# Decode attention of the sample rows: between the blocks of the gating branch instead of behind the heads of the recurrence

## The chip, the cores and the metric

The kernel runs on one core of one Trainium2 chip, in one launch. The metric is the device time of a run in microseconds. Engines are called by the profile's names: PE is TensorE (PEld its weight loads), DVE is VectorE, ACT is ScalarE, POOL is GpSimd, and SP is SyncE, whose queue issues most of the DMAs.

## What is computed

The reference is one step of a decoder layer with three parallel branches over one input projection. A prompt of 1024 tokens and 8 sample rows (one new token for each of 8 sequences) go through the same layer:

```python
h = rms(x, norm_g); proj = h @ w_in
aq, ak, av, az, bu, bv, bz, cq, cf, ci, cz = split(proj)
o_a = dilated attention          # windows (128,1), (512,4), (2048,16), mixed by softmax denominators
o_b = bu * (tril(W_s) @ layernorm(bv) + b)      # gating in chunks of 128
o_c = rms(HGRN2 recurrence of cq, cf, ci)       # 6 heads, state 128 x 128
x + concat(o_a * silu(az), o_b * silu(bz), o_c * silu(cz)) @ w_out
```

For the sample rows, the attention is a decode step: each of the 8 new queries meets up to 129 keys of each of the three patterns, gathered by stride from a cache of 2048 rows, and its own new key:

```python
kg, vg = kk[:, idx], vv[:, idx]                 # idx = W + t - arange(win // dil + 1) * dil
s = einsum('bthe,btnhe->bthn', q, kg); p, lse = softmax_stats(s)
out = combine over the patterns of einsum('bthn,btnhe->bthe', p, vg)
```

It needs the projections of the sample rows and the caches, and nothing of the other two branches. Its result is needed by the output projection of the sample rows alone.

## The kernel before, in words

Everything is unrolled. The order on each engine and each DMA queue is not written by hand: the framework takes the program's order as a priority, runs a simulated timeline, and lets an engine take the first instruction that is ready in it. The result is a fixed order for each engine and each queue; on the chip an engine that waits holds up all that is behind it in that order. Tiles come from pools by tag; each tag has a fixed number of buffers, and a new tile waits until an older one of the tag has been read for the last time.

The stages in the order of the program are: input norm and transposes; `attention()` (three rounds of two head pairs); `hgrn()`, the recurrence; `sgu()`, the gating branch; `out_proj(U)`, four blocks of 256 output columns with eight row tiles of 128 tokens each.

`hgrn()` (from line 780) goes over three pairs of heads. Per pair it projects the values (`c_proj_i`), the queries and forget gates of the first head (`c_proj_qf`, also of the second head further down) and the output gates z (`c_proj_z`). Per head follow `c_head`, which computes the prompt's recurrence (three levels of decay-weighted products by `levels`, tiles T, masked into `cmat` by lines 722 to 729), `c_step` (line 763), which advances the state of the 8 sample rows, and `decode` (line 923). A projection collects 24 matmuls in one of two PSUM banks (tag "proj"); for q and z a bank is emptied by `gate`, whose first instruction is on DVE (line 152). So projections of the next head or pair fill PE while DVE works on the current head, as long as DVE comes to the gates.

`decode(p)` handles one of six pairs of attention heads. Per half of the batch it loads the queries, broadcast to all partitions (`dqb`, line 947), and three tiles of gathered keys (`dk`, line 935; one more small load for the new key, line 937). DVE multiplies (line 949) and reduces (line 950) each tile into the score tile `dsc`. A maximum follows over partitions by way of two small transposes (`pmx`, `pmb`), then exponential, multiplicities, denominator (`pdn`), the weighted sum of six value tiles on PE (`pda`, 48 matmuls), a transposition (`pdt`) and the last multiply into `ysT` (line 978). The tiles dqb, dk, dv and the copy for the transposition have the tag "pq" with five buffers, which `c_step` (vb, ss), `sgu` (two rows of norm weights) and `out_proj` (xr, line 1036) use as well. The score tile has one buffer, tag "dsc", cleared by two memsets on POOL (lines 943, 944). PSUM tiles of decode share the one bank of tag "tr" with c_step and a few transposes of sgu.

`sgu()` (line 811) transposes and masks W_s with `triu`, adds up bias terms `bT`, projects v in two blocks (`bv`, row statistics in `st6`, which has the tag "dsc" too), normalises, and then runs four blocks of projections, bz 0, bu 0, bz 1, bu 1 (lines 885 to 899), with the mixing matmuls (`mx`) after each bu. Each block begins with `load_w` (line 192): four loads of 256 KB on SP's queue, a rounding copy on ACT and a subtraction on POOL (line 206) for the low half.

`out_proj` loads the columns `y` and `yb` from DRAM, `xr` per row tile, and adds the PSUM result to xr on DVE (line 1054). PE's sample rows (`pos`, `pon`) need ysT of all six decodes.

Of the kernel before, what the change touches and what calls it, by code (L numbers as in the profile page):

```python
# [18 lines left out]
P = 128  # L19
# [3 lines left out]
NT = S // P  # L23
# [11 lines left out]
OFF_BU, OFF_BV, OFF_BZ = 3072, 3584, 4096  # L35
# [4 lines left out]
NEG = -3.0e38  # L40
# [51 lines left out]
def hybrid_step(tc, ins, outs, parts=("A", "D", "B", "C", "O"), dbg=None):  # L92
    nc = tc.nc
# [8 lines left out]
    with tc.tile_pool(name="const", bufs=1) as cp, tc.tile_pool(name="sb", bufs=1) as sb, \  # L102
# [14 lines left out]
        def s2b(nm, dt=F32, shape=(P, 512)):  # L117
            return sb.tile(list(shape), dt, tag="s2b", name=nm, bufs=N_S2B)
# [4 lines left out]
        def small(nm, n, p=P, dt=F32, bufs=2, tag=None):  # L123
            return sb.tile([p, n], dt, tag=tag or f"sm{n}", name=nm, bufs=bufs)
# [94 lines left out]
        for t in (0, NT, *range(1, NT)):  # L219
# [15 lines left out]
            for j in range(2):  # L235
                ps = p_st(f"tr0_{t}_{j}").rearrange("p (a b) -> p a b", a=4)
                for i in range(4):
                    k = 4 * j + i
# [541 lines left out]
        def hgrn():  # L780
            cm = sb.tile([P, 1024], F32, tag="mask", name="cmat", bufs=1)
            lmask, dmask = cm[:, 640:856].bitcast(BF16), cm[:, 856:872].bitcast(BF16)
            nc.gpsimd.dma_start(lmask, ins["lmask"])
            nc.gpsimd.dma_start(dmask, ins["dmask"])
            nc.gpsimd.memset(cm[:, 512:640], 0.0)
            At = [(cm[:, 256 * j:256 * j + 256], cm[:, 512 + 64 * j:576 + 64 * j]) for j in range(2)]
            for hp in range(3):
                V = c_proj_i(hp)
                a = c_proj_qf(2 * hp)
                Z = c_proj_z(hp)  # L790
                c_head(2 * hp, *a, V[0], Z[0], At, lmask, dmask)
                c_step(2 * hp, *a)
                decode(2 * hp)
                a = c_proj_qf(2 * hp + 1)
                c_head(2 * hp + 1, *a, V[1], Z[1], At, lmask, dmask)
                c_step(2 * hp + 1, *a)
                decode(2 * hp + 1)

            n = HC * NS
            sq = pq("ssq", (P, n))  # L800
            nc.scalar.activation(sq, osT.rearrange("p h b -> p (h b)"), AF.Square)
            pn = p_tr("pns")
            mm(pn[:, :n], ones, sq, True, True)
            nc.scalar.activation(sq, pn[:, :n], AF.Ln, scale=1.0 / P, bias=eps)
            nc.scalar.activation(sq, sq, AF.Exp, scale=-0.5)
            nc.vector.tensor_tensor(osT, osT, sq.rearrange("p (h b) -> p h b", b=NS), ALU.mult)
            nc.vector.tensor_tensor(osT, osT, gn[:, :, None].to_broadcast([P, HC, NS]), ALU.mult)
            nc.vector.tensor_tensor(ysT[:, 10:16, :], osT, zsT, ALU.mult)


        def sgu():
            triu = small("triu", P, bufs=1, tag="kg")
            nc.scalar.dma_start(triu, ins["triu"])
            wn = wk("wn", (P, 8, P))
            nc.scalar.dma_start(wn, ins["sgu_w"][0].rearrange("g t s -> t g s"))
# [19 lines left out]

            vraw = [inp(f"vraw{g}", (P, 2, CB)) for g in range(4)]
            v_s = s2b("v_s", shape=(NS, CB))
            st6 = small("st6", NT * 12, bufs=1, tag="dsc").rearrange("p (t a b) -> p t a b", t=NT, a=2)
            for j in range(2):
                blk = load_w([(OFF_BV + j * NW, NW)], f"bv{j}")  # L840
                st = proj_nat_s(blk, f"bv{j}")
                nc.scalar.copy(v_s[:, j * NW:(j + 1) * NW], st)
                for g in range(4):
                    ps = p_proj(f"pbv{j}_{g}").rearrange("p (a b) -> p a b", a=2)
                    for i in range(2):
                        proj_nat(blk, 2 * g + i, ps[:, i, :])
                    dst = vraw[g][:, :, j * NW:(j + 1) * NW]
                    nc.scalar.copy(dst, ps)
                    for i in range(2):
                        nc.vector.bn_stats(st6[:, 2 * g + i, j, :], dst[:, i, :])  # L850
# [16 lines left out]
            for nm, op in (("sgu_ln_g", ALU.mult), ("sgu_ln_b", ALU.add)):  # L867
                t = pq(f"s_{nm}", (NS, CB))
# [16 lines left out]
            U = []  # L885
            for j in range(2):
                U += [inp(f"u{j}_{i}") for i in range(2)]
                for nm, off in (("bz", OFF_BZ), ("bu", OFF_BU)):
                    blk = load_w([(off + j * NW, NW)], f"{nm}{j}")
                    for i in range(2):  # L890
                        for c in range(3):
                            ps = p_proj(f"p{nm}{j}_{i}_{c}")
                            proj_T(blk, i * P, c, ps[:, :TC])
                            us = U[2 * j + i][:, c * TC:(c + 1) * TC]
                            if nm == "bz":
                                gate(us, ps[:, :TC], f"bzt{j}_{i}_{c}")
                            else:
                                nc.vector.tensor_tensor(us, ps[:, :TC], us, ALU.mult)
# [21 lines left out]
            cns[nm] = cp.tile(list(ins[nm].shape), F32, name=nm)  # L920
            tc.keep_in_program_order(nc.scalar.dma_start(cns[nm], ins[nm]))

        def decode(p):

            ROWS = ((P, 1920, 1), (96, 1536, 4), (96, 0, 16))
            ch = slice(p * P, (p + 1) * P)
# [11 lines left out]
                        n += 1  # L938
                    yield kind, n, t

            scw = small(f"dsc{p}", 138, bufs=1, tag="dsc").rearrange("p (k a) -> p k a", k=3)
            sc = scw[:, :, 0:16]
            nc.gpsimd.memset(sc, NEG)
            nc.gpsimd.memset(scw[:, :, 16:], 0.0)
            for bb in range(2):
                qb = dk(f"dqb{p}_{bb}")
                nc.sync.dma_start(qb, qkv_d[0, 4 * bb:4 * bb + 4, ch].partition_broadcast(P))
# [118 lines left out]
        if "A" in parts:  # L1066
            attention()
        if "C" in parts:
            hgrn()
        if "B" in parts:  # L1070
            U = sgu()
        if "O" in parts:
            out_proj(U)

# [23 lines left out]
```

## Time and profile before

| | |
|---|---|
| median of 3 runs | 1285.43 us (1284.22 to 1287.84) |
| the profiled execution, its own time | 1283.54 us |
| its span from the first to the last instruction | 1281.8 us |
| mean granted TensorE clock | 0.977 |
| share of the span: PE, DVE, ACT, POOL busy | 94%, 71%, 52%, 23% |
| chain that ended last | PE 72%, DVE 16%, DMA 5% |
| DMA | 114.17 MB, 89 GB/s |

The span is cut into stages by what runs in them: attention until some 560 us, the recurrence's heads until 996 us, the gating branch until 1084 us, then the output projection. Stages overlap at their edges. Busy time of an engine says little by itself; the gaps of PE and what ended them say where time is lost. The granted clock is the share of full speed at which PE was allowed to run in a stretch.

### The profile page before, as it was taken

What the parts mean: (1) busy time and instruction counts of PE and PEld (TensorE: products, weight loads), DVE (VectorE), ACT (ScalarE), POOL (GpSimd) and SP (SyncE); (2) the same over time, 40 slices, a digit from 0 to 9 for tenths busy, and PEclk for the clock granted to TensorE, in tenths of its full rate; (3) what the DMA queues carried; (4) which work ended last, traced back from release to release, by engine and by line L of the source; (5) the groups of instructions that cost most, each with busy time, mean ns of one, the idle gap of its engine ahead of it and who ended that gap; (6) DMA issues with size and microseconds to landing.
All of it is one profiled execution on the core that took longest, in us unless ns stands there. A gap on an engine that the chain in (4) does not pass through costs nothing.

```text
span 1281.8 us, 27727 instructions
## 1 busy us (share of the span) xinstructions
PE 1206.7 (94%) x10610; PEld 1119.9 (87%) x10610; DVE 914.1 (71%) x2425; ACT 669.8 (52%) x1512; POOL 290.1 (23%) x272
## 2 busy tenths in 40 slices
PE   3899999999999998998999889998999999999998
PEld 2899888998899988987988878887989899899998
DVE  4845888668876786789897898989796534654643
ACT  5445554765547565575445554665443252455543
POOL 4431201312203221122012121111011254122221
PEclk9999999999899998999999889999999999999999
DMA  7241222312223141142253514424253224621110
GB/s 224 68 136 34 65 55 79 108 37 66 71 67 100 42 117 52 25 111 84 67 146 92 131 46 139 127 80 112 81 149 97 84 75 137 194 80 47 62 47 29
DMA packets 165044, 114.17 MB, mean 89 GB/s; under 512 B 13944, under 2 KB 158992, under 8 KB 164912
## 3 DMA queue, kind: packets, MB, share of 16 engines
q1 hardware_dynamic: 157520, 110.28, 29.4%
q10 hardware_dynamic: 6816, 1.54, 0.6%
q8 instruction: 83, 1.36, 0.4%
q0 software_dynamic: 576, 0.58, 0.3%
q14 instruction: 49, 0.40, 0.1%
HBM read 84.47 MB, written 22.09 MB: 83 GB/s over the span
## 4 chain that ended last, share of the span: by engine, by line
PE 72%; DVE 16%; DMA 5%; issue 3%; ACT 3%; SPq 0%; POOL 0%; ACTq 0%; POOLq 0%; DVEq 0%
PE po L100 15%; PE pqk L100 10%; PE pv L100 9%; PE paz L100 5%; PE pi L100 4%; PE pbu L100 4%; PE pbz L100 4%; PE pcz L100 4%; PE pc L100 3%; PE pbv L100 3%; PE st L100 3%; DMA dk<-in_cache_k_dram 2%; PE s L100 2%; DVE T L647 1%; DVE T L649 1%
## 5 line engine op out<-in xcount | busy, mean ns | idle before, releaser
L100 PE MATMUL pqk<-wh_qk,h 128*128 128x256 f32 x768 | 156.6, 294 | 9.1 <-DVE h L243 4.4
L100 PE MATMUL pc<-h,wh_cqf 128*128 128x344 f32 x576 | 144.6, 331 | 10.3 <-DVE cz L152 8.8
L100 PE MATMUL po<-woh,yl 128*128 128x256 f32 x512 | 144.5, 283 | 0.0
L100 PE MATMUL po<-woh,yh 128*128 128x256 f32 x512 | 144.1, 282 | 0.3 <-ACT yh L1046 0.3
L100 PE MATMUL po<-wol,yh 128*128 128x256 f32 x512 | 143.9, 281 | 0.0
L100 PEld LDWEIGHTS pqk<-wh_qk,h 128*128 128x128 f32 x768 | 127.9, 198 | 17.0 <-DVE h L243 5.0
L100 PEld LDWEIGHTS pc<-h,wh_cqf 128*128 128x128 f32 x576 | 102.1, 194 | 13.4 <-DVE cz L152 9.7
L100 PE MATMUL pqk<-wl_qk,h 128*128 128x256 f32 x384 | 112.1, 292 | 0.0
L100 PEld LDWEIGHTS po<-woh,yl 128*128 128x128 f32 x512 | 96.6, 189 | 3.0 <-issue 1.7
L100 PEld LDWEIGHTS po<-woh,yh 128*128 128x128 f32 x512 | 96.3, 188 | 2.1 <-ACT yh L1046 2.1
L100 PEld LDWEIGHTS po<-wol,yh 128*128 128x128 f32 x512 | 96.5, 189 | 0.0
L100 PE MATMUL pc<-h,wl_cqf 128*128 128x344 f32 x288 | 95.3, 333 | 0.0
L455 DVE CUSTOM_DVE_ANT_0 s<-s,masks 128x512 f32<-128x512 f32 (+2 forms) x144 | 77.6, 576 | 19.4 <-PE s L100 18.6
L100 PE MATMUL pi<-wh_ci,h 128*128 128x256 f32 x384 | 79.1, 301 | 10.5 <-DVE cmat L722 8.1
L100 PEld LDWEIGHTS pqk<-wl_qk,h 128*128 128x128 f32 x384 | 75.7, 197 | 1.4 <-issue 0.2
L100 PEld LDWEIGHTS pi<-wh_ci,h 128*128 128x128 f32 x384 | 65.1, 204 | 13.6 <-ACT dsc L962 5.4
L100 PE MATMUL pv<-wh_v,h 128*128 128x256 f32 x384 | 75.2, 287 | 1.0 <-ACT den L516 1.0
L100 PE MATMUL pcz<-h,wh_cz 128*128 128x344 f32 x288 | 71.2, 325 | 0.2 <-DVE q L152 0.2
L100 PE MATMUL paz<-h,wh_az 128*128 128x344 f32 x288 | 68.9, 323 | 0.0
L1047 DVE TENSOR_TENSOR yl<-yb,yh 128x512 fp32r<-128x512 f32 x44 | 30.3, 692 | 52.6 <-ACT yh L1046 52.6
L100 PEld LDWEIGHTS pv<-wh_v,h 128*128 128x128 f32 x384 | 61.1, 189 | 3.1 <-ACT st L493 1.1
L1046 ACT CAST yh<-yb 128x512 fp32r<-128x512 f32 x64 | 39.5, 620 | 42.7 <-PE po L100 41.9
(389 smaller groups left out, 3586.5 us busy)
## 6 DMA issues: line engine op xcount, KB each, us to landing
wro<-in_w_out_dram SPq DMA_DIRECT2D x32, 256.0 KB
wr_qk<-in_w_in_dram SPq DMA_DIRECT2D x48, 128.0 KB
wr_cqf<-in_w_in_dram SPq DMA_DIRECT2D x48, 128.0 KB
dk<-in_cache_k_dram SPq DMA_DIRECT2D x24, 192.0 KB
dv<-in_cache_v_dram SPq DMA_DIRECT2D x24, 192.0 KB
xt<-in_x_prompt_dram SPq DMA_DIRECT2D x8, 512.0 KB
xr<-in_x_prompt_dram SPq DMA_DIRECT2D x32, 128.0 KB
out_o_yp_dram<-xr SPq DMA_DIRECT2D x32, 128.0 KB
```

The costliest lines, as they stand in the source:

```text
L100: nc.tensor.matmul(out, lhsT=lhsT, rhs=rhs, start=start, stop=stop)
L455: nc.vector.tensor_tensor_reduce(out=ps[:, :w], in0=ps[:, :w], in1=nmask[:, S - n + c:S - n + c + w], op0=ALU.add, op1=ALU.max, scale=1.0, ...
L647: nc.vector.tensor_tensor(K.rearrange("p (n w) -> p n w", w=w), g3[:, :, w - 1:w].to_broadcast([P, 4 * n, w]), h3, ALU.subtract)
L649: nc.vector.tensor_tensor(Q[:, 0:3], g4[:, 1:4], g4[:, 0:3, :, w - 1:w].to_broadcast([P, 3, n, w]), ALU.subtract)
L1046: nc.scalar.copy(yh[:, sl, :], y)
L1047: (nc.gpsimd if piece == 0 else nc.vector).tensor_tensor(yl[:, sl, :], y, yh[:, sl, :].bitcast(F32), ALU.subtract)
```

## The change

The calls of `decode` leave `hgrn()`. In `sgu()`, decode 0 and 1 are called ahead of the two bv blocks, and decode 2 to 5 ahead of the blocks bz 0, bu 0, bz 1, bu 1. Decodes of odd number take their score tile from 138 unused columns of the tile `cmat`, which `hgrn` now returns, instead of the one buffer of "dsc"; the two memsets of the scores go from POOL to DVE; `triu` moves to a buffer of the tag "s2b" (two buffers, also used for kT, csq, v_s, ms and tb), and `st6` to the buffer of "kg" that triu had.

```diff
--- before.py
+++ after.py
@@ -790,11 +790,9 @@
                 Z = c_proj_z(hp)
                 c_head(2 * hp, *a, V[0], Z[0], At, lmask, dmask)
                 c_step(2 * hp, *a)
-                decode(2 * hp)
                 a = c_proj_qf(2 * hp + 1)
                 c_head(2 * hp + 1, *a, V[1], Z[1], At, lmask, dmask)
                 c_step(2 * hp + 1, *a)
-                decode(2 * hp + 1)
 
             n = HC * NS
             sq = pq("ssq", (P, n))
@@ -806,10 +804,11 @@
             nc.vector.tensor_tensor(osT, osT, sq.rearrange("p (h b) -> p h b", b=NS), ALU.mult)
             nc.vector.tensor_tensor(osT, osT, gn[:, :, None].to_broadcast([P, HC, NS]), ALU.mult)
             nc.vector.tensor_tensor(ysT[:, 10:16, :], osT, zsT, ALU.mult)
-
-
-        def sgu():
-            triu = small("triu", P, bufs=1, tag="kg")
+            return cm[:, 872:1010]
+
+
+        def sgu(wide):
+            triu = s2b("triu", shape=(P, P))
             nc.scalar.dma_start(triu, ins["triu"])
             wn = wk("wn", (P, 8, P))
             nc.scalar.dma_start(wn, ins["sgu_w"][0].rearrange("g t s -> t g s"))
@@ -835,8 +834,9 @@
 
             vraw = [inp(f"vraw{g}", (P, 2, CB)) for g in range(4)]
             v_s = s2b("v_s", shape=(NS, CB))
-            st6 = small("st6", NT * 12, bufs=1, tag="dsc").rearrange("p (t a b) -> p t a b", t=NT, a=2)
+            st6 = small("st6", NT * 12, bufs=1, tag="kg").rearrange("p (t a b) -> p t a b", t=NT, a=2)
             for j in range(2):
+                decode(j, wide)
                 blk = load_w([(OFF_BV + j * NW, NW)], f"bv{j}")
                 st = proj_nat_s(blk, f"bv{j}")
                 nc.scalar.copy(v_s[:, j * NW:(j + 1) * NW], st)
@@ -885,7 +885,8 @@
             U = []
             for j in range(2):
                 U += [inp(f"u{j}_{i}") for i in range(2)]
-                for nm, off in (("bz", OFF_BZ), ("bu", OFF_BU)):
+                for jj, (nm, off) in enumerate((("bz", OFF_BZ), ("bu", OFF_BU))):
+                    decode(2 + 2 * j + jj, wide)
                     blk = load_w([(off + j * NW, NW)], f"{nm}{j}")
                     for i in range(2):
                         for c in range(3):
@@ -920,7 +921,7 @@
             cns[nm] = cp.tile(list(ins[nm].shape), F32, name=nm)
             tc.keep_in_program_order(nc.scalar.dma_start(cns[nm], ins[nm]))
 
-        def decode(p):
+        def decode(p, wide):
 
             ROWS = ((P, 1920, 1), (96, 1536, 4), (96, 0, 16))
             ch = slice(p * P, (p + 1) * P)
@@ -938,10 +939,10 @@
                         n += 1
                     yield kind, n, t
 
-            scw = small(f"dsc{p}", 138, bufs=1, tag="dsc").rearrange("p (k a) -> p k a", k=3)
+            scw = (wide if p % 2 else small(f"dsc{p}", 138, bufs=1, tag="dsc")).rearrange("p (k a) -> p k a", k=3)
             sc = scw[:, :, 0:16]
-            nc.gpsimd.memset(sc, NEG)
-            nc.gpsimd.memset(scw[:, :, 16:], 0.0)
+            nc.vector.memset(sc, NEG)
+            nc.vector.memset(scw[:, :, 16:], 0.0)
             for bb in range(2):
                 qb = dk(f"dqb{p}_{bb}")
                 nc.sync.dma_start(qb, qkv_d[0, 4 * bb:4 * bb + 4, ch].partition_broadcast(P))
@@ -1066,9 +1067,9 @@
         if "A" in parts:
             attention()
         if "C" in parts:
-            hgrn()
+            wide = hgrn()
         if "B" in parts:
-            U = sgu()
+            U = sgu(wide)
         if "O" in parts:
             out_proj(U)
```

## Rows read from the trace of the kernel before

**Rows 1.** The page's first part: busy us, share of the span, instructions.

```profile
PE 1206.7 (94%) x10610; PEld 1119.9 (87%) x10610; DVE 914.1 (71%) x2425; ACT 669.8 (52%) x1512; POOL 290.1 (23%) x272
```

**Rows 2.** Busy time by stage: stretch, length, PE, PEld, DVE, ACT, POOL, PEclk, DMA share, GB/s.

```profile
565.00:645.00 80.00, 71.75 (x780) 65.76 (x778) 72.31 (x206) 45.82 (x114) 18.19 (x16) 0.94 0.34 93
645.00:717.00 72.00, 68.69 (x724) 63.15 (x724) 60.58 (x166) 38.69 (x85) 14.88 (x12) 1.00 0.43 120
...
996.00:1084.00 88.00, 88.00 (x623) 81.48 (x624) 34.54 (x62) 28.02 (x57) 37.82 (x29) 1.00 0.29 88
565.00:996.00 431.00, 399.24 (x4390) 365.66 (x4389) 369.64 (x1100) 224.67 (x542) 73.67 (x62) 0.96 0.38 105
```

**Rows 3.** PE's waits, 480 to 1110 us: who waited for whom, us, times, longest.

```profile
PE pc L100 <- DVE cz L152: 8.8, 3, 3.7
PE pi L100 <- DVE cmat L722: 8.1, 2, 5.0
...
PE pss_bv L100 <- DVE q L152: 3.3, 1, 3.3
...
PE pss_ci L100 <- DVE q L152: 1.4, 2, 0.9
PE pmx L955 <- DVE dmx L953: 1.3, 1, 1.3
...
PE pcz L100 <- POOL wl_cz L206: 0.7, 1, 0.7
```

**Rows 4.** Busy time of three 10 us windows inside heads 0, 2 and 4.

```profile
600.00:610.00 10.00, 6.42 (x45) 5.21 (x44) 9.97 (x28) 8.32 (x18) 7.55 (x4) 0.80 0.32 91
...
750.00:760.00 10.00, 5.54 (x28) 5.57 (x29) 9.88 (x33) 6.08 (x14) 3.81 (x3) 0.66 0.36 106
890.00:900.00 10.00, 6.17 (x38) 4.69 (x39) 9.87 (x29) 6.49 (x15) 3.35 (x3) 0.66 0.32 107
```

**Rows 5.** Decode's DVE instructions, by tile: ns min/median/max, first and last start.

```profile
L949 DVE TENSOR_TENSOR dk<-dk,dqb x36: 670/682/694, 577.4 to 945.5; 128x512 f32<-128x512 f32 x12, 97x512 f32<-97x512 f32 x12, 96x512 f32<-96x512 f32 x12
L950 DVE TENSOR_REDUCE dsc<-dk x36: 664/673/686, 579.6 to 947.3; 128x8 f32<-128x512 f32 x12, 97x8 f32<-97x512 f32 x12, 96x8 f32<-96x512 f32 x12
...
L967 DVE RECIPROCAL dmx<-pdn x6: 239/242/257, 617.2 to 963.3; 128x16 f32<-128x16 f32 x6
L978 DVE TENSOR_TENSOR ysT<-ysT,dmx x6: 157/159/162, 638.3 to 985.0; 128x8 f32<-128x8 f32 x6
```

**Rows 6.** Busy time of the instructions on dv, 560 to 1010 us, their sum.

```profile
sum 450.00, PE 13.55 PEld 8.07; mean PE 0.30 PEld 0.18
```

**Rows 7.** POOL's wait before the memset of the scores: us, times, longest.

```profile
POOL dsc L943 <- PE pda L100: 55.4, 4, 22.4
```

**Rows 8.** The same DVE operation of `levels` at two moments (start, us).

```profile
604.47 1.08 DVE L654 TENSOR_TENSOR T<-T,dec 128x64 f32<-128x64 f32 x1
...
758.77 0.20 DVE L654 TENSOR_TENSOR T<-T,dec 128x64 f32<-128x64 f32 x1
```

**Rows 9.** Two users of the tag "s2", by tile: first and last start.

```profile
L827 ACTq DMA_DIRECT2D bT<-in_sgu_b_dram x8: 472/604/1053, 973.4 to 980.4; - x8
...
L649 DVE TENSOR_TENSOR T<-G x72: 331/352/1460, 565.7 to 955.7; 128x192 f32<-128x192 f32 x72
```

**Rows 10.** SP's queue around decode 5, a landing time in the chain, and xr's addition.

```profile
928.32 1.46 SPq L947 DMA_DIRECT2D dqb<-qkv_scr  x1
...
966.78 0.38 SPq L935 DMA_DIRECT2D dv<-in_cache_v_dram  x1
...
981.03 8.18 SPq L1036 DMA_DIRECT2D xr<-in_x_prompt_dram  x3
...
1079.86 10.75 SPq L1015 DMA_DIRECT2D yb<-y_scr  x7
...
644.36 5.16 DMA dk<-in_cache_k_dram
...
L1054 DVE TENSOR_TENSOR xr<-xr,po x32: 400/421/422, 1091.7 to 1278.5; 128x256 f32<-128x256 f32 x32
```

## The prediction

> **What bounds the kernel now.** The first thing read is the page's busy line: TensorE (PE) works 1206.7 us of a 1281.8 us span [rows 1], so the most that any reordering can win without removing work is the 75 us in which PE idles, plus what it loses at the lower clock. The table by stage comes next, to see where those 75 us lie [rows 2]. From 565 to 996 us, the heads of the recurrence, PE works 399.24 of 431 us and the granted clock is 0.96; from 996 to 1084 us, the gating branch, PE is never idle while VectorE (DVE) works only 34.54 of 88 us. The reader should see two things there: the recurrence holds 31.8 us of PE idleness, with DVE busy 369.64 of 431 us; and the loss is uneven. The stretch of head 0 (565 to 645) loses 8.3 us, that of head 1 (645 to 717) 3.3 us. PE's own list of waits then says what ended the idleness [rows 3]: 8.8 us at the start of a first head of a pair (projection matmuls behind the DVE gate of z), and in the middle of such a head 8.1 + 3.3 + 1.4 = 12.8 us, where a projection's PSUM bank waits for DVE. Three 10 us windows at these middles show DVE at 9.9 of 10 us, PE at 5.5 to 6.4 us, and a granted clock of 0.80, 0.66 and 0.66 [rows 4]. So this stage is bound by DVE in bursts, and PE pays for it twice, by idling and by running at the lower of its two levels, 1.2 instead of 2.4 GHz, afterwards.
>
> **The change part by part.**
> *DVE work leaves the recurrence.* Per decode six multiplies of 0.682 and six reductions of 0.673 us [rows 5], 8.1 us, and ten small operations between 0.16 and 0.24 us like the last column multiply and the reciprocal, about 2 us: 10 us a decode, 60 us in six. Five of six go behind the last head; the sixth ran during the last head and decode 0 will too. In head 0 the decode's multiplies and reductions ran ahead of the middle burst, on a DVE that was saturated from there to the burst. Without them DVE reaches the gate that PE waits for some 8 us earlier, and the 12.8 us fall on three such bursts, 4.3 us each on average, so I take them all as gone, and the 1.3 us that PE waited for a decode's maximum [rows 3]. The bounds are 1.3 us (only the decode's own wait) and 31.8 us (every idle microsecond of the stage).
> *Clock.* At 0.80, 0.66 and 0.66 of 10 us, PE was at the lower level for 4.0 + 6.8 + 6.8 = 17.6 us. If all of it fell on matmuls, half of it, 8.8 us, was lost; where it fell on idle time, nothing. I take 3 us. The sum for the recurrence is -12.8 - 1.3 - 3 = -17 us.
> *The start of each pair stays.* The 8.8 us behind the gate of z come before the decode's first multiply, so they are not in my sum.
> *PE work is moved, not removed.* The 288 matmuls of the weighted sum take 13.55 us of PE [rows 6], the transposes and the denominator some 3 us. They leave a stage and enter another, both limited by PE most of the time: nothing in the sum. In the gating branch PE has no idle time to hide them in; they lengthen it by the 16 us by which they shorten the recurrence.
> *Score clearing goes from POOL to DVE, and a second score tile is used.* POOL stood 55.4 us in four waits for the previous decode's matmuls [rows 7]; behind it in POOL's queue are the low halves of the weights. PE's list names POOL for 0.7 us [rows 3], so what this frees is priced at nothing; it is covered by PE's other work. On DVE twelve clears enter; by the nearest DVE row, the reciprocal of 0.242 us, they are 2.9 us of a DVE that idles 53 of 88 us. If the second tile's predecessor is still being read, a clear on DVE blocks all DVE behind it, the gates of bz above all; with two tiles in turn the reader is two decodes back, so I take nothing.
> *Port sharing.* In the window where POOL ran four subtractions in 7.55 us [rows 4], DVE's 128x64 multiply took 1.08 us, against 0.20 us elsewhere [rows 8]. In the gating branch POOL is busy 37.82 of 88 us against 73.67 of 431 [rows 2], so the moved multiplies, which read two operands, will be stretched more often; at worst 36 x 0.88 = 32 us, still within DVE's idle 53 us, so the sum gets nothing. The Trainium skill (SBUF — State Buffer, section "SBUF: two separate sides") says that a VectorE operation with two SBUF inputs and a GpSimd operation that reads SBUF take a shared port pair in turn, each for its whole length. That rule speaks against this change, since it moves such operations to where GpSimd is busier; the trace agrees with it by the 1.08 us, and by it the sum would still be the same.
> *Other tiles.* triu moves to the tag of kT and csq and so behind the last head's, and the statistics tile st6 leaves the score tile's tag, whose last reader was decode 5. Both are priced at nothing: PE has the bz block to work on meanwhile; if that cover is gone, the cost is the load of triu, some 5 us like a cache load's [rows 10].
> *Loads.* Each decode has two query loads, twelve cache loads and four small ones on SP's queue, and 15 tiles pass through the five "pq" buffers. Buffers of a tag seem to be given out in program order: bT, ready from the start, was loaded at 973.4 us, after the last T tile of the same tag was begun at 955.7 [rows 9]. Then decode 0 starts once the sample step of the last head has its buffers, and the output projection's xr tiles, of the same tag, come behind decode 5. In the old order decode 5 issued its first load at 928.32 and its last at 966.78, 38.5 us apart, finished at 985.0 [rows 5], and xr was loaded from 981, 110 us before its first use [rows 10]. That lead vanishes. Weight loads are issued on the same SP queue; with six raw buffers they run a block and a half ahead, which covers a decode load that waits for its buffer.
> *Is there room for six?* The third tile of the output projection needs xr 0, since its matmuls have two PSUM banks and the first must be emptied. A tile takes (1278.5 - 1091.7) / 31 = 6.0 us [rows 10]; so xr must land 12 us after 1084, and be issued 5 us before, the time that a cache load took to land [rows 10], so at 1091. From 928 that is 163 us, plus the 13 us of PE work of five decodes that no longer lie ahead: 29 us for each of six. If the sample step of the last head, which had waited for decode 4's buffers, runs up to 30 us earlier, it is 34 us. I take 37 us for decode 0 under the last head's DVE load, 33 for decode 1, and 27 for the rest, where DVE is idle more than half the time: 178 us in all against 176 to 206. It just fits, without margin.
> *Price behind the recurrence.* Between nothing and the 50 us that six decodes of 38.5 us would be late (231 - 176 = 55). I take 4 us, nearer to nothing since it fits, for a start of the output projection that is crowded: SP already needs 10.75 us there to issue seven y loads [rows 10].
> *Sum.* -17 + 4 = -13 us. The profiled execution took 1283.54 us, so 1270.5; the median of the runs shown is 1.9 us above it. I say 1271.
>
> **The rivals.**
> 1. *Slower: the decodes don't fit.* The place is the third tile of the output projection, where PE waits for xr behind decode 5 in the "pq" buffers, while SP's queue is full of y loads. It decides if a decode takes more than about 34 us on average. At the 38.5 us seen before it is late by 25 to 55 us; with 30, the time is 1283.5 - 17 + 30 = 1296. For it: the only pitch that the trace shows is 38.5 us, each decode passes one-buffer tiles ("tr", "dmx"), and its start is held by the last sample step. Against: that pitch was measured with DVE busy 9 of 10 us, and behind 996 us DVE is mostly free.
> 2. *No change: the backlog is not the decode's.* The heads' own level and mask operations fill DVE in the bursts, and another of them takes the place of each decode operation; then only 1.3 us and a little clock are won and 2 to 4 are paid behind: 1283 to 1286. For it: at the waits themselves DVE runs level operations, not decode ones, some stretched by POOL. Against: odd heads, with the same operations, lose little.
> 3. *All of the stage's idleness goes.* With POOL free and the sample step early, DVE has 60 us more, and the starts of the pairs relax too: 1283.5 - 31.8 = 1252.
>
> **How the numbers follow.** Forecast 0.5, rival 1 0.23, rival 2 0.15, rival 3 0.12. A measurement of this kernel tells about 0.3% from no change, 3.9 us. Faster: rival 3 and nearly all of the forecast's cases (some end within 3.9 us): 0.61. Same: rival 2 mostly, and the edge of the forecast: 0.16. Slower: 0.23. The range reaches down to rival 3's 1252 and up to 1294, leaving out the upper half of rival 1 and what lies beyond rival 3; the forecast's own range is 1260 to 1280.
>
> **What would show it.** In the changed profile the middles of heads 0, 2 and 4 should show PE busy 9 to 10 of 10 us at a clock near 1.0, the recurrence should be 25 to 35 us shorter (17 from waits, the rest moved PE work) and the gating branch some 14 us longer, with PE still without idle time. POOL's wait for the weighted sum should be gone. Decode 5's last load should be issued before PE begins the output projection's third tile. I am wrong if PE's list of waits has a new entry of over 5 us at the output projection's DVE addition or its xr loads (rival 1), or if the waits behind DVE in the middle of the first heads stand as before (rival 2).

## The result, and the profile after

The changed kernel takes 1344.86 us, median of four runs (1342.36 to 1348.83), against 1284.83 us for the kernel before in the same comparison (1280.58 to 1287.84): a ratio of 1.048, 95% interval 1.0452 to 1.0507. It is 60 us slower. The forecast was 1271, the range ended at 1294, and slower had a chance of 0.23. The profiled execution took 1348.83 us; its span is 1347.0 us and the mean granted clock 0.953 (before: 1281.8 us and 0.977).

First the page's busy line and two lines of its picture in 40 slices, of the kernel after; the first answers to [rows 1].

```profile
PE 1223.3 (91%) x10610; PEld 1131.3 (84%) x10610; DVE 917.8 (68%) x2437; ACT 673.4 (50%) x1512; POOL 292.8 (22%) x260
...
PE   4899999998999989988998799889999953899999
...
PEclk9899999999999989989999999999999875799999
```

The matmuls are the same 10610, but PE is busy 16.6 us longer and its span is 65.2 us longer, so 48.6 us are new idleness. The picture shows where: one hole in slices 33 to 35, where the granted clock falls to 0.5 of full speed.

A table by stage makes that exact. The stages are cut at the first matmul of the recurrence (`pi`), of the gating branch (`pbv`) and of the output projection, and at the last matmul. Columns as in [rows 2]: stretch, length, busy us of PE, PEld, DVE, ACT and POOL, granted clock, DMA share, GB/s. The kernel before, cut in the same way:

```profile
462.80:896.00 433.20, 398.27 (x3904) 365.74 (x3902) 362.58 (x972) 239.43 (x546) 77.00 (x65) 0.96 0.34 95
896.00:1082.90 186.90, 184.83 (x1760) 171.19 (x1760) 113.52 (x348) 70.77 (x167) 48.16 (x38) 0.98 0.33 98
1082.90:1278.40 195.50, 195.10 (x1695) 186.37 (x1694) 110.46 (x263) 97.82 (x246) 43.76 (x32) 1.00 0.27 85
```

The kernel after:

```profile
464.00:880.00 416.00, 384.29 (x3686) 359.56 (x3685) 314.80 (x885) 241.74 (x543) 74.82 (x57) 0.96 0.22 64
880.00:1073.50 193.50, 185.10 (x1770) 172.66 (x1770) 137.39 (x371) 69.52 (x163) 49.46 (x35) 0.97 0.40 115
1073.50:1343.60 270.10, 224.08 (x1906) 201.33 (x1902) 140.23 (x337) 100.30 (x253) 47.34 (x35) 0.88 0.34 101
```

The recurrence became 17.2 us shorter, the gating branch 6.6 us longer, and the output projection **74.6 us longer**: 64.0 us, and another 1.2 us lie ahead of the recurrence. Reading the recurrence's line closely already shows that the gain isn't the one that was forecast: PE's busy time fell by 14.0 us (moved work), its idle time only from 34.9 to 31.7 us.

What happens in the output projection stands in PE's list of waits (who waited for whom, us, times, longest), in a window over the hole, in SP's queue and in a timeline of PE (start, duration, what, and in brackets the idle time before it and what ended it).

```profile
PE pmx L956 <- DVE dmx L954: 21.6, 3, 8.6
...
PE pc L100 <- DVE cz L152: 11.1, 3, 3.7
PE pi L100 <- ACT V L621: 8.2, 3, 3.4
PE pi L100 <- DVE q L152: 6.1, 2, 3.0
...
PE pbv L100 <- DVE q L152: 3.0, 1, 3.0
```

```profile
1094.70:1157.00 62.30, 23.48 (x221) 11.46 (x219) 30.43 (x77) 3.36 (x11) 0.00 (x0) 0.53 0.57 160
```

```profile
1109.44 0.38 SPq L948 DMA_DIRECT2D dqb<-qkv_scr  x1
...
1129.05 0.38 SPq L948 DMA_DIRECT2D dqb<-qkv_scr  x1
...
1149.34 4.08 SPq L1037 DMA_DIRECT2D xr<-in_x_prompt_dram  x5
```

```profile
1124.13 0.37 PE L956 MATMUL pmx<-ident,dmx 128*16 128x128 f32 x1 [8.58 <-DVE dmx L954]
1125.12 0.28 PE L961 MATMUL pmb<-ident,dmb 16*128 16x16 f32 x1 [0.62 <-DVE dmb L959]
1126.55 0.58 PE L100 MATMUL pdn<-dmx,ones 128*128 128x16 f32 x2 [1.15 <-DVE dmx L965]
1127.48 2.36 PE L100 MATMUL pda<-dv,dsc 128*32 128x128 f32 x40 [0.35 <-DVE dmx L968]
1131.71 0.65 PE L100 MATMUL pda<-dv,dsc 96*32 96x128 f32 x8 [1.87 <-DMA dv<-in_cache_v_dram]
1132.86 0.69 PE L759 MATMUL pdt<-ident,pdt4s 128*128 128x128 f32 x2 [0.49 <-ACT pdt4s L756]
```

For 62.3 us PE has nothing but the remaining decodes and the products of the sample rows that depend on them, 23.48 us in all, at a clock of 0.53, which is nearly the lower level of 1.2 GHz throughout. The output projection has filled its two PSUM banks and can't begin its third tile, since xr 0 isn't there; xr 0 is asked for at 1149.34, at once when decode 5 gives its "pq" buffers back (before: 981 [rows 10]). The first use of xr comes at 1153.6 and the third tile begins at 1157.02. The waits of this stretch are booked under the decodes' products (`pmx` 21.6 us), because in PE's fixed order these stand ahead of the third tile; an entry at xr, the sign that the prediction named, doesn't appear in the list. This is the place and the mechanism of the first rival. Its size isn't: 25 to 55 us late had been worked out, and the time of that rival was 1296.

The second thing to read is why decode 5 was so late. The transposes that close a decode (`pdt`) start at 1010.0, 1043.5, 1094.8, 1112.4, 1132.9 and 1152.3 us, and decode 0 issued its first load at 892.8. So decode 0 alone took 117 us. Five rows, by line (min/median/max ns, first and last start), name what it stood behind:

```profile
L954 DVE TENSOR_REDUCE dmx<-dsc x3: 184/198/208, 923.5 to 1123.8; 128x16 f32<-128x48 f32 x3
```

```profile
L956 PE MATMUL pmx<-ident,dmx x6: 270/320/372, 988.5 to 1144.4; 128*16 128x128 f32 x6
```

```profile
L818 PE MATMUL wtp<-ident,wn x8: 271/272/273, 907.2 to 978.5; 128*128 128x128 f32 x8
```

```profile
L820 DVE TENSOR_TENSOR wn<-wtp,triu x2: 660/676/692, 973.6 to 979.2; 128x512 f32<-128x512 f32 x2
```

```profile
L812 ACTq DMA_DIRECT2D triu<-in_triu_dram x1: 348/348/348, 971.8 to 971.8; - x1
```

Decode 0's maximum is ready at 923.5, and the transpose that needs it runs at 988.5, 65 us later. Both it and the transposes of W_s write the one PSUM bank of the tag "tr". The preparation of W_s stands ahead of decode 0 in program order; its first four transposes took the bank at 907.2, and the mask that empties it ran at 973.6, because triu, now in the tag of the last head's kT and csq, was loaded at 971.8. The other four transposes (from 978) and the row sums `rs`, which are read out until 986.4, followed in the same bank, and then came decode 0. Behind a load of 65 KB (128 x 128 values of 4 bytes) lay the whole chain of decodes.

### The profile page after: what moved, and what is told of

Read it like the earlier page. It is cut to its first block, busy times and chain, and to the rows that moved or that the text cites. A ratio compares the mean times of both kernels' runs of the same rounds, so it can differ in the third digit from the quotient of the medians.

```text
span 1347.0 us, 27762 instructions
## 1 busy us (share of the span) xinstructions
PE 1223.3 (91%) x10610; PEld 1131.3 (84%) x10610; DVE 917.8 (68%) x2437; ACT 673.4 (50%) x1512; POOL 292.8 (22%) x260
## 5 line engine op out<-in xcount | busy, mean ns | idle before, releaser
L100 PE MATMUL po<-woh,yh 128*128 128x256 f32 x512 | 147.2, 288 | 4.9 <-ACT yh L1047 4.9
L100 PEld LDWEIGHTS po<-woh,yh 128*128 128x128 f32 x512 | 97.8, 191 | 11.7 <-ACT yh L1047 8.8
```

Of the source, the lines that this page charges most:

```text
L100: nc.tensor.matmul(out, lhsT=lhsT, rhs=rhs, start=start, stop=stop)
```

## The experiments

Theory at the start: three causes in a row, (1) the preparation holds the bank of decode 0, (2) the decodes then run late into the output projection, (3) xr, behind them in the same buffers, stops PE. And the stalls of the recurrence were never the decodes'. Rivals: that some other buffer holds decode 0; that a decode is slow by itself beside these stages; that the waits of the recurrence did move.

**1. triu out of the late buffer.** The free columns of the mask tile hold it:

```diff
-            triu = s2b("triu", shape=(P, P))
+            triu = wide[:, 0:P]
```

> The changed kernel, with triu held in the first 128 of the 138 spare columns of cmat (free until decode 1) instead of a buffer of the tag s2b. Theory (bank): in the changed kernel the first four transposes of W_s take the only PSUM bank of the tag tr at 907 us and keep it until 973.6, because triu comes behind the last head's kT and csq in s2b; decode 0's maximum, ready at 923.5, waits for that bank until 988. With triu early, decode 0 ends some 60 us earlier, and the last xr load moves from 1149 to about 1090 to 1105: 1285 to 1300 us. Rival (buffers): five pq buffers and the loads set the pace anyway, and decode 0 being early only makes the next ones wait elsewhere: 1325 to 1345 us.

Measured: 1339.29 us, ratio 1.0442 (1.0404 to 1.048). That is the rival's figure, and the trace says why: the eight transposes now ran at 902 to 909 us, but the next user of the bank took their place.

```profile
L833 DVE SCALAR_TENSOR_TENSOR bT<-rs,lnw,bT x4: 341/345/350, 964.8 to 970.2; 128x128 f32<-128x128 f32 x4
```

```profile
L826 ACTq DMA_DIRECT2D bT<-in_sgu_b_dram x8: 472/607/1346, 959.5 to 965.4; - x8
```

The row sums `rs` hold the bank until bT is loaded, and bT is behind the last head's T tiles, as it had been before [rows 9]. Freeing one of two late buffers in a row wins 5.6 us. So the bank theory wasn't decided by this run.

**2. xr out of the decodes' buffers**, into the two of the gates:

```diff
-                    xr = pq(f"xr{nb}_{t}", (P, NW))
+                    xr = small(f"xr{nb}_{t}", NW, tag="gt", bufs=N_GT)
```

> The changed kernel, with the output projection's xr tiles in the two buffers of the tag gt (free after the last gate) instead of pq behind decode 5. Theory (order of buffers): PE's stand from 1095 to 1157 us comes from xr queued behind the decodes; with it gone PE goes on with the output projection while decodes 3 to 5 run beside it, 1280 to 1295 us. Rival (decode's own results): PE stands because its fixed order puts the sample rows' matmuls and the decodes' small matmuls there, and these wait for the decodes all the same: over 1320 us.

Measured: 1306.76 us, ratio 1.0188 (1.0156 to 1.0219). The long stand is gone: that one dependency was worth 38 us. The time is 12 us over the expected span. Decodes 3 to 5 now close beside the output projection, at 1126.3, 1161.5 and 1192.7; what each of them costs there was not separated.

**3. Both edits.**

> Both edits: triu in the spare columns of cmat and xr in the tag gt. If the two causes are all that went wrong, no long stand is left and the time is that of the kernel before less what the recurrence won: 1270 to 1285 us. If decode beside PE-bound stages costs by itself (loads against the y and weight loads, in-order waits), 1290 to 1310 us.

Measured: 1302.62 us, ratio 1.0154 (1.0122 to 1.0186). The upper of the two spans held.

**4. The kernel before without its decodes**, so without the sample rows' attention.

```diff
-                decode(2 * hp)
...
-                decode(2 * hp + 1)
```

> The kernel before without the six decodes: the sample rows' attention output is left out (ysT keeps only the gates there). It gives the most that any placement could win. The decode's PE work is about 16 us. If the recurrence's stalls in the middle of first heads come from the decode's DVE work (the forecast), they go too: 1240 to 1252 us. If they do not (second rival), only the PE work and the few direct waits go: 1262 to 1270 us.

Measured: 1262.41 us, ratio 0.9839 (0.9807 to 0.9872). Its recurrence (columns as above) and PE's waits:

```profile
461.10:876.50 415.40, 383.97 (x3686) 359.69 (x3684) 314.42 (x883) 241.62 (x543) 74.56 (x57) 0.96 0.22 64
```

```profile
PE pc L100 <- DVE cz L152: 11.3, 3, 3.9
PE pi L100 <- ACT V L621: 7.6, 3, 3.4
PE pi L100 <- DVE q L152: 6.1, 2, 3.0
...
PE pbv L100 <- DVE q L152: 3.0, 1, 3.0
```

This run settles the recurrence. With no decode anywhere its PE idles 31.4 us, as much as in the changed kernel (31.7), and the waits are the same ones of the same length. The recurrence of the changed kernel is as long as one without decodes (416.0 and 415.4 us), so what leaving the recurrence can win there was won, and it is mostly the moved PE work. The run also prices the decodes in the kernel before: 21.5 us of the median, with 20.3 us less busy time of PE (1206.7 against 1186.4 on the two pages). So 21.5 us is the most that placing them elsewhere could win, and nearly all of it would need their products to run in gaps in which PE idles anyway.

**5. The preparation behind the two blocks of bv**, so that nothing holds the bank while decodes 0 and 1 run. The block from `triu` to the loop that fills `bT` moves as it is:

```diff
         def sgu(wide):
-            triu = s2b("triu", shape=(P, P))
-            nc.scalar.dma_start(triu, ins["triu"])
...
             vraw = [inp(f"vraw{g}", (P, 2, CB)) for g in range(4)]
...
                         nc.vector.bn_stats(st6[:, 2 * g + i, j, :], dst[:, i, :])
+            triu = s2b("triu", shape=(P, P))
+            nc.scalar.dma_start(triu, ins["triu"])
...
```

> The changed kernel with the preparation of W_s, triu and the bias (transposes, mask, row sums) put behind the two blocks of bv, so that no part of it can hold the one bank of tag 'tr' while decode 0 and 1 run. Bank theory (decode 0 was late because the preparation held the bank while it waited for buffers of the last head): the max transpose of decode 0 comes within 5 us of its scores, near 925 instead of 988, decode 5 is done near 1095 instead of 1149, the stand at out_proj's start falls from 62 us to under 20, and the time is 1290 to 1315. Rival (a decode in these stages takes its 40 us and more by itself, whatever holds the bank): decode 0 ends after 970 and the time stays over 1325.

Measured: 1315.45 us, ratio 1.024 (1.0211 to 1.0269), 29 us less than the changed kernel, by order alone.

```profile
L954 DVE TENSOR_REDUCE dmx<-dsc x3: 184/185/199, 920.0 to 1076.3; 128x16 f32<-128x48 f32 x3
```

```profile
L956 PE MATMUL pmx<-ident,dmx x6: 270/278/372, 920.3 to 1109.0; 128*16 128x128 f32 x6
```

The transpose runs 0.1 us after the maximum instead of 65 us: the bank theory holds. But the time lies just over the upper edge of the expected span. Decode 5's closing transpose comes at 1116.8 and the first xr load at 1113.9, not near 1095, and a stand of 28 us is left ahead of the third tile (1094.3 to 1122.4), where under 20 was expected: each decode still takes long.

**6. The same, with xr in the gates' buffers.**

> The same, and out_proj's residual tiles in the buffers of the gates instead of those of the decodes' cache tiles. If bank and residual were the whole of the loss, 1268 to 1285, level with the kernel before or better. If decoding beside stages that TensorE fills costs by itself (lone 128x16 and 32-column products, and the products of the sample rows of out_proj pushed behind decode 5), 1290 to 1303, about what the kernel with triu and residual moved gave.

Measured: 1291.47 us over ten runs, ratio 1.0054 (1.0034 to 1.0073), in the span of a decode that costs by itself. The two edits together take back 53 of the 60 us. They overlap: the preparation's move is worth 29 us in the changed kernel and 15 once xr is out of the way (run 2 to this one). Its stages:

```profile
464.00:879.50 415.50, 382.90 (x3685) 358.28 (x3684) 314.68 (x885) 241.62 (x543) 74.81 (x57) 0.97 0.22 64
879.50:1079.80 200.30, 192.03 (x1875) 176.16 (x1875) 149.24 (x410) 70.10 (x167) 50.02 (x37) 0.98 0.50 140
1079.80:1288.70 208.90, 206.29 (x1801) 191.30 (x1798) 123.71 (x298) 99.75 (x249) 46.01 (x33) 1.00 0.34 103
```

Against before, PE's busy time is 15.4 us less in the recurrence and 7.2 + 11.2 = 18.4 us more behind it: the work has moved and grown a little. Idle time is 2.3 us less in the recurrence and 6.2 + 2.2 us more behind it. Freed of its two waits, the change is close to neutral, a little to the wrong side.

This kernel also shows what paces a decode. Its `pdt` start at 944.5, 988.1, 1032.6, 1069.2, 1105.0 and 1140.8 us, 52 us after decode 0's first load and then 44, 44, 37, 36 and 36 us apart, with no bank held for long. One decode from its maximum to its last transpose, on PE:

```profile
1045.68 0.27 PE L956 MATMUL pmx<-ident,dmx 128*16 128x128 f32 x1
1050.58 0.23 PE L961 MATMUL pmb<-ident,dmb 16*128 16x16 f32 x1
1056.37 0.29 PE L100 MATMUL pdn<-dmx,ones 128*128 128x16 f32 x2
1060.34 1.31 PE L100 MATMUL pda<-dv,cmat 128*32 128x128 f32 x40
1065.23 0.43 PE L100 MATMUL pda<-dv,cmat 96*32 96x128 f32 x8
1069.16 0.38 PE L759 MATMUL pdt<-ident,pdt3s 128*128 128x128 f32 x2
```

Set this beside the same six steps in the hole of the changed kernel, shown above: 23.5 us from `pmx` to `pdt` here, 8.7 us there, although PE ran the steps there at the lower clock (the 40 products of `pda` took 2.36 us, here 1.31). Here no bracket follows a row, since PE never stood: it was busy with the projections, and small products stood in line behind theirs. `pmb` had its operand at 1046.51 and ran at 1050.58; `pdn` 1054.71 and 1056.37; `pda` 1057.45 and 1060.34; `pdt` 1066.11 and 1069.16. These four stands are 11.7 us, most of the 14.8 us of difference; another 2.2 us went by until VectorE came to the subtraction behind `pmb`. In the hole the closing transposes of decodes 3 to 5 are 20 us apart, here 36. So the rival that a decode is slow by itself beside these stages holds too.

**7. The two rows of the layer norm for the sample rows out of "pq" as well** (in halves, in the gates' buffers).

```diff
-                t = pq(f"s_{nm}", (NS, CB))
+                for hf in range(2):
+                    t = small(f"s_{nm}{hf}", NW, NS, tag="gt", bufs=N_GT)
```

> The same, and the two rows of the gating branch's layer norm for the sample rows taken in halves from the gates' buffers too, so that nothing but the decodes is left in the ring of cache tiles. If that order (the rows behind decode 1) delays the mixing of the gating branch, 5 to 10 us less than the kernel with the residual moved; if the mixing waits for something else, within 3 us of it.

Measured: 1296.63 us, ratio 1.0091 (1.0066 to 1.0115). Neither span held: the mixing's first products came 3 us sooner (994.9 against 997.7), and the time is 5 us longer than in run 6, not shorter. So the order of those rows isn't a cause of the loss. Why it is longer wasn't followed up.

**8. Only decodes 4 and 5 moved**, to before the second block of bv and the first of bz.

```diff
-                decode(2 * hp)
+                if hp < 2:
+                    decode(2 * hp)
...
             for j in range(2):
+                if j:
+                    decode(4)
                 blk = load_w([(OFF_BV + j * NW, NW)], f"bv{j}")
...
+                if j == 0:
+                    decode(5)
                 for nm, off in (("bz", OFF_BZ), ("bu", OFF_BU)):
```

> The kernel before with only decodes 4 and 5 moved: 4 ahead of the second block of bv, 5 ahead of the first block of bz; 0 to 3 stay behind heads 0 to 3 and triu in its early buffer. If the loss is a matter of room (six decodes do not fit between the blocks, two do), within 6 us of the kernel before, 1278 to 1290. If each moved decode costs by itself (18 us over six: 3 us each), 1288 to 1294. If the waits of the recurrence were its own, as the kernel without decode said, the recurrence of this one is shorter by the two decodes' busy time alone, some 7 us.

Measured: 1291.76 us over ten runs, ratio 1.0051 (1.0029 to 1.0072): 8 us over the kernel before, within the span of 3 us per moved decode and outside that of "room". No stand appears (its decodes are done at 1043.9). The recurrence did not get shorter (434.4 us from the first `pi` to the first `pbv`, before 433.2), and the trace shows why: in the kernel before 192 of the 288 products of the weighted sums lie ahead of 896 us and 96 behind, so the sums of two of its six decodes already ran beside bv and bz, and moving them moved no work out. On the two pages PE's busy time grew by 7.5 us (1214.2 against 1206.7) with the same number of products, and the span by 8.6, so most of the loss is products that take longer, not idle time. It is spread: 2.7 us in the recurrence, 1.5 in the gating branch, 3.4 behind it. The products of the sample rows (`pon` and `pos`, counted once where they overlap) are busy for 16.3 us here, 12.3 before, and 14.9 in the kernel without decodes. Why the products take longer stays open.

**9. Run 5 without the maximum in the decodes**: two of the chain's products and the steps around them are left out.

```diff
-            pt = p_dk(f"pmx{p}")
-            nc.tensor.transpose(pt[0:16, 0:P], mx[:, 0:16], ident)
...
-            pt2 = p_dk(f"pmb{p}")
-            nc.tensor.transpose(pt2[:, 0:16], mb[:, 0:P], ident[0:16, 0:16])
-            nc.vector.tensor_tensor(sc, sc, pt2[:, None, 0:16].to_broadcast([P, 3, 16]), ALU.subtract)
```

> The kernel with the preparation put late (1315 us), and in the decodes the maximum and its subtraction left out (two of the six products of the chain, and two copies on VectorE). If the pitch of a decode is made by its chain of products standing in line behind the projections' products (24 us from the maximum to the last transpose beside them, 9 us with TensorE free), two steps fewer bring each decode's pitch from about 38 to 28 to 32, the residual loads come from 1114 to 1080 at the latest, the stand before them goes, and the time is 1288 to 1298. If the pitch is made by the loads of the cache tiles through their five buffers, it stays at 36 and more, and the time within 5 us of 1315.

Measured: 1300.53 us, ratio 1.0113 (1.0088 to 1.0139): 15 us less than run 5, 2.5 us over the expected span. The first xr load comes at 1106.5, not by 1080, and PE still goes through decode 5 alone for 10 us ahead of the third tile (1104.9 to 1114.8, 6.49 us busy). The closing transposes:

```profile
1023.77 0.44 PE L759 MATMUL pdt<-ident,pdt2s 128*128 128x128 f32 x2
1051.08 0.38 PE L759 MATMUL pdt<-ident,pdt3s 128*128 128x128 f32 x2
1080.92 0.38 PE L759 MATMUL pdt<-ident,pdt4s 128*128 128x128 f32 x2
1110.13 0.44 PE L759 MATMUL pdt<-ident,pdt5s 128*128 128x128 f32 x2 [0.49 <-ACT pdt5s L756]
```

Beside bz, bu and the output projection the pitch (the time from one decode's closing transpose to the next one's) fell to 27 to 30 us, against 36 to 37 in run 6, from which this one otherwise differs in the place of xr alone. Against its own base, run 5, decode 3 can be compared, which closes ahead of the stand: 36.6 us there, 27.3 here. Two steps fewer are 6 to 9 us less. There the length of the chain sets the pitch, and the rival in its pure form (the loads' five buffers, whatever the chain) falls. Whether more buffers would let the next decode begin while a chain is still running was not tried. Beside bv and the preparation it hardly moved: from decode 0 to decode 2 it takes 83 us here and 88 in runs 5 and 6. For decode 2 the rows show the bank once more:

```profile
1002.63 1.03 PE L100 MATMUL rs<-wn,ones 128*64 128x512 f32 x4
1008.46 0.41 PE L881 MATMUL pst<-ident,ms 8*128 8x8 f32 x4
1012.22 0.29 PE L100 MATMUL pdn<-dmx,ones 128*128 128x16 f32 x2
```

```profile
1001.99 0.19 DVE L956 TENSOR_REDUCE dmx<-dsc 128x16 f32<-128x48 f32 x1
```

The sums were ready at 1002.2, but `rs` held the bank until bT was formed from it (1006.0) and `pst` until its copy (1009.1); `pdn` followed at 1012.2. The preparation put late had become an obstacle of decode 2 instead of decode 0. What slows decode 1 was not taken apart.

**10 to 12. Three parts of the change alone, in the kernel before**: the memsets on VectorE; triu in the late buffer; xr in the gates' buffers.

```diff
-            nc.gpsimd.memset(sc, NEG)
-            nc.gpsimd.memset(scw[:, :, 16:], 0.0)
+            nc.vector.memset(sc, NEG)
+            nc.vector.memset(scw[:, :, 16:], 0.0)
```

> The kernel before with only the two memsets of each decode put on VectorE. Priced at nothing: within 4 us of the kernel before by both theories. A time over 1290 would mean that waits of VectorE on the score tile cost the recurrence something.

Measured: 1282.94 us, ratio 0.9995 (0.9978 to 1.0012).

```diff
-            triu = small("triu", P, bufs=1, tag="kg")
+            triu = s2b("triu", shape=(P, P))
```

> The kernel before with only triu in the buffer of the last head's tiles, decodes where they were. Its preparation of W_s then holds the bank until about 975 as in the changed kernel, but of the decodes only the last is still to come. If the late buffer costs only through the decodes behind it: within 5 us of the kernel before. If it costs by itself through the mixing of the gating branch: 1290 to 1300.

Measured: 1282.53 us, ratio 0.9982 (0.9965 to 0.9999). The premise on the bank was off: decode 5 is ahead of the preparation in this order, so triu was loaded at 992.8 and the transposes ran from 991.5 to 999.4, and nothing came behind them that was in a hurry.

```diff
-                    xr = pq(f"xr{nb}_{t}", (P, NW))
+                    xr = small(f"xr{nb}_{t}", NW, tag="gt", bufs=N_GT)
```

> The kernel before with only the residual tiles of out_proj in the two buffers of the gates. Within 4 us of the kernel before by every theory: the loads are asked for one tile ahead and take 2 to 5 us of a tile's 6. More than that would be the price of two buffers for five, and belongs to the kernels in which the residual was moved.

Measured: 1283.17 us, ratio 0.9989 (0.997 to 1.0007).

None of the three costs anything by itself. The preparation ahead of the decodes, with its late triu and bT, and the shared "pq" buffers, harmless in the kernel before, cost 29 and 38 us, each removed alone from the changed kernel, and 53 together.

No version that keeps the decodes is faster than the kernel before by more than 0.2% (run 11). By run 4 the decodes' own waits are worth some 1 to 3 us; the rest of the 21.5 us is work of PE, and a placement that hides it in PE's gaps was not tried. Nor was a bank of their own for the decodes.

## Why the prediction was wrong, step by step

**The waits of the recurrence: wrong.** The step that failed is "the 12.8 us fall on three such bursts, so I take them all as gone". They didn't go with the decodes. Before, the waits behind DVE at these heads were 8.8 + 8.1 + 3.3 + 1.4 us [rows 3], and another 3.4 us were behind ACT's copies of V; without any decode they are 11.3 + 6.1 + 3.0 us behind DVE and 7.6 behind ACT. At the three middles the changed kernel waits 9.1 us for DVE's gate of q, where 12.8 were, and in heads 0 and 2 another 6.2 us for ACT some 11 us later. The names changed; the idle time of the stage is 31.4 us without any decode and 34.9 with them. That is the second rival's mechanism, the backlog of the heads themselves, which had 0.15. The windows at the middles of heads 0, 2 and 4 [rows 4] had shown DVE full and a decode's work running before; that doesn't say that the wait ends sooner without it. Taking the decodes out made DVE 48 us less busy in this stage (362.58 to 314.80), and one such window of the kernel after still reads:

```profile
740.00:750.00 10.00, 6.97 (x66) 6.08 (x65) 9.97 (x21) 6.60 (x13) 4.93 (x4) 1.00 0.36 106
```

PE was to be busy 9 to 10 of these 10 us. The 1.3 us of `pmx` did go, and idle time fell by 3.2 us in all: the lower bound was close.

**The clock: nothing of it can be seen.** This row is at 1.00, but the ten microseconds behind it are at 0.83, and so they are in the kernel without decodes. The dips are shallower than the 0.66 of before [rows 4], yet the stage's mean is 0.96 in both kernels. The 3 us that were taken for it are not in the result.

**The recurrence 25 to 35 us shorter, 17 of it from waits: wrong.** It is 17.2 us shorter, but 14.0 of these are PE work that moved out and had to be paid behind; from waits come 3.2. That the total equals the forecast's 17 is chance.

**PE work is moved, not removed: right, and a little more came back than left.** 16 us were estimated; the kernel without decodes has 20.3 us less busy time, and in run 6 15.4 us left the recurrence and 18.4 came back. The gating branch didn't stay without idle time: PE idles 8.4 of its 193.5 us.

**triu and bT "priced at nothing; if that cover is gone, some 5 us": wrong.** The cover was looked for on PE, which did have other work. What stood behind the load was not PE but the bank "tr", and with it decode 0, all decodes after it, and xr. That decodes pass the one-buffer tag "tr" was named in the first rival; that the preparation holds it ahead of them was not. Its price, by run 5, is 29 us, and by run 1 triu alone is worth 5.6 of them, since bT kept the bank. The rule that would have pointed there is in the Trainium skill (Perfetto Trace Analysis, section "Matmuls"): independent groups of matmuls should rotate through different PSUM banks, so that emptying one overlaps the next. Here two independent groups had one bank, and the 65 us between decode 0's maximum and its transpose agree with it.

**"37 us for decode 0, 33 for decode 1, and 27 for the rest ... it just fits": wrong, and the chief miss of size.** 178 us were forecast. With the bank free and no stand (run 6) it is 248.5 us, 41 on average, where 34 was the point of decision; in the changed kernel, from 892.8 to xr at 1149.3, 256.5. The estimate took the pitch from VectorE's free time, below the only figure that the trace showed, 38.5 us. That figure ran from a decode's first load to its last; to its closing transpose the same decode took 52.6 us (928.3 to 980.9), as long as decode 0 of run 6. VectorE had room (137.39 of 193.5 us busy in the gating branch), but what paces a decode there is mostly the row of six products in PE's queue: 23.5 us beside the projections against 8.7 with PE idle. The stage was chosen for VectorE's room; it is one in which PE never waits, and so the links of the chain wait for PE.

**The price behind the recurrence, 4 us within 0 to 50: wrong.** The output projection's stage alone is 74.6 us longer. The upper bound counted the lateness of xr but neither the bank's 65 us nor that decode work in the stand runs at the lower clock, nor the work that stays beside the output projection once xr is free (run 2, still 22 us over before).

**The first rival: right in place and mechanism**, PE at the third tile, xr behind decode 5 in "pq". The hint in [rows 9], that buffers of a tag are given out in program order, was read for xr and not followed for triu.

**What was priced at nothing and was nothing:** the memsets on VectorE and POOL's freed queue (run 10). The premise that a clear on DVE finds its tile free was off: in the changed kernel DVE stands 9.6 us in three clears, behind the weighted sum two decodes back, the longest 4.8 us; the second score tile was not tested alone. The moved multiplies went from a median of 682 [rows 5] to 690 ns, the longest from 694 to 1762; all 36 together went from 24.6 to 29.0 us, which VectorE had to spare.

**What stays open:** the 8 us of run 8, and what run 7 added to run 6. What run 6 still loses is seen in its profiled execution as 3 us more PE work and 6 us more idle time, not traced link by link.

## What to carry to other kernels

Work that is moved takes its place in every queue and every buffer it uses: for each tag and each PSUM bank, list who holds it ahead of the moved work and what that holder waits for, and who stands behind it; here two harmless tenants became a chain of 65 us and a stand of 62. Before pricing an idle gap as won, take the suspected work out altogether and see whether the gap goes. Time a chain of small dependent steps by the queue of the engine that each step must pass, not by the free time of the engine that does most of its work.

## What the runs showed of the hardware

The same chain of six small products took 23.5 us from first to last where PE was fully busy and 8.7 us where PE stood idle between them, even though in the idle stretch the granted clock was 0.5 and the 40 products of `pda` took 2.36 us instead of 1.31. The products of the sample rows in the output projection, 160 in number and 379 ns each at their shortest in every kernel, overlap one another. Counted once where they do, they keep PE busy for 12.3 us in the kernel before, 14.9 without decodes and 20.3 in the changed kernel, where those at the lower clock last up to 634 ns each. How much of that PE loses to them is not shown, since other products run in the same spans. And 48 us less work for VectorE in a stage where it is busy 84% of the time bought 3 us.
